# The last tile in parts of 384 and 128 tokens, and 1/rms from a square root and one Newton step

## The chip, the cores and the metric

The program runs on one NeuronCore of a Trainium2 chip. The metric is the device time of one execution in microseconds (us), as the median of several. Engines are named as in the profile: PE (TensorE, matrix products), PEld (its weight loads), DVE (VectorE), ACT (ScalarE), POOL (GpSimd) and SP (SyncE, which here only issues DMAs).

## The reference, cut to what matters

Two decoder layers over 512 tokens of 1024 features: a gated linear recurrence, a convolutional feed-forward block, differential attention over shared keys and values, a second feed-forward block, and a final RMS norm. The change touches only the very end: the last down-projection, the residual sum and the norm.

```
x = x + conv_ffn(rmsnorm(x, norm_ffn[1]), ffn_w_up[1], ...)   # ends in  hidden (512 x 2816) @ w_down (2816 x 1024)
return rmsnorm(x, final_norm)                                 # y = x * rsqrt(mean(x*x, axis=-1) + 1e-6) * g
```

## The kernel before

All arrays lie feature by token: the stream `x` is eight tiles `x[0..7]` of 128 features by T = 512 tokens. Products are in three terms (`mm3`, L104 to L106): each operand is split into a high and a low part (`whi`/`wlo` of a weight, `hh`/`hl` of the hidden layer), and high by high, high by low and low by high are added in one PSUM bank. Each of the three is a matmul with its own weight load.

The second feed-forward block ends in `residual`: for each output tile n it multiplies KF = 22 hidden tiles by 22 blocks of weights, so 66 matmuls of 128x512. The sum is added to `x[n]` (L543), squared on ACT (L148) and accumulated into `acc` on DVE. For the last tile, n = 7, `last_tile` is called. It holds everything that has to follow the last product, and cuts it by tokens so that the first part's norm and stores run under the second part's product:

- `product(half, ks)`: the matmuls of one part for the hidden tiles `ks`. Each part is 66 matmuls, here of 128x256.
- `squares(half)`: residual sum on DVE (L589), squares on ACT (L590), and `scaled` (L585), which multiplies x by the norm's gain into `xg`.
- `sums`: sums over features, as matmuls of a 128-token column block against a column of ones (L183); a column of the result is the sum of one 128-token chunk, a token to a partition. `before` holds the sums over the first seven tiles, already scaled by 1/D with EPS added (L648).
- `factor(half)`: 1/rms on DVE for two columns: the mean square (L603), an integer seed (L604), -0.5 times the mean square (L605), then three Newton steps of `r*mh*r` (L611) and `(u+1.5)*r` (L614), column by column.
- `spread(r)`: each column is turned into a row that all partitions share, by a transpose on PE (L188), into two PSUM banks.
- `finish(half, rb)`: ACT copies one of the two banks to SBUF (L629, `rbc_fin`); DVE multiplies the tiles it has (L634) from the other bank and POOL the rest (L632) into `fin`; each pair of tiles goes to `out` by a DMA (L637), on SP's queue, for the second half on SP's and ACT's in turn.

Inside `manual_schedule(engines=ORDERED)` PE, DVE, ACT and POOL run in the order in which the code is written; SP's DMAs, and how the block is merged with the loop ahead of it, are ordered by the framework's own scheduler. On each engine instructions run in order.

Of the kernel before, what the change touches and what calls it, by code (L numbers as in the profile page):

```python
# [11 lines left out]
F32 = mybir.dt.float32  # L12
F32R = mybir.dt.float32r
I32 = mybir.dt.int32
AF = mybir.ActivationFunctionType
ALU = mybir.AluOpType
# [3 lines left out]
P = 128  # L20
T = 512
D = 1024
KD = D // P
# [3 lines left out]
EPS = 1e-6  # L27
# [9 lines left out]
class Trunk:  # L37
# [527 lines left out]
    def last_tile(self, w_src, ys, kt, acc, out):  # L565

        nc, v, sp = self.nc, self.nc.vector, self.sp
        ws = []
        for k0 in range(0, kt, 8):
            wd = min(8, kt - k0)  # L570
            ws.append(self.weights(w_src[:, k0 * P:(k0 + wd) * P], wd * P))
        x, last = self.x, KD - 1
        t = [slice(half * 256, half * 256 + 256) for half in range(2)]
        ps = [self.bank() for _ in range(2)]
        sq = [sp.tile([P, T], F32, tag="sq", name="sq", bufs=2) for _ in range(2)]

        def product(half, ks):
            for k in ks:
                hi, lo = ws[k // 8]
                c = slice(k % 8 * P, k % 8 * P + P)  # L580
                self.mm3(ps[half][:, :256], (hi[:, c], lo[:, c]), (ys[k][0][:, t[half]], ys[k][1][:, t[half]]),
                         k == 0, k == kt - 1)

        def scaled(n, c):
            nc.scalar.activation(xg[n][:, c], x[n][:, c], AF.Identity, scale=self.gain(5, n))  # L585

        def squares(half):
            c = t[half]
            v.tensor_tensor(x[last][:, c], x[last][:, c], ps[half][:, :256], ALU.add)  # L589
            nc.scalar.activation(sq[half][:, c], x[last][:, c], AF.Square)  # L590
            scaled(last, c)

        def tmp(dt=F32):
            return sp.tile([P, 4], dt, tag="rs", name="rs", bufs=18)[:, :2]

        def sums(src, half):
            return self.sums(src, "mm", (2 * half, 2 * half + 1))[:, 2 * half:2 * half + 2]

        def factor(half):

            ss = sums(sq[half], half)
            ms, mh, i = tmp(), tmp(), tmp(I32)
            v.scalar_tensor_tensor(ms, ss, 1.0 / D, before[half], ALU.mult, ALU.add)  # L603
            v.tensor_scalar(i, ms.bitcast(I32), -0.5, float(0x5F3759DF), ALU.mult, ALU.add)  # L604
            v.tensor_scalar(mh, ms, -0.5, None, ALU.mult)  # L605
            r = i.bitcast(F32)
            for step in range(3):
                u, rn = tmp(), tmp()
                for c in range(2):
                    c = slice(c, c + 1)  # L610
                    v.scalar_tensor_tensor(u[:, c], r[:, c], mh[:, c], r[:, c], ALU.mult, ALU.mult)  # L611
                for c in range(2):
                    c = slice(c, c + 1)
                    v.scalar_tensor_tensor(rn[:, c], u[:, c], 1.5, r[:, c], ALU.add, ALU.mult)  # L614
                r = rn
            return r

        def spread(r):

            both = [self.bank() for _ in range(2)]  # L620
            for rb in both:
                for c in range(2):
                    self.by_column(rb[:, c * P:(c + 1) * P], r[:, c:c + 1])
            return both

        def finish(half, rb):
            by_pool = (KD - 2, KD - 1) if half else (KD - 3, KD - 2, KD - 1)
            rs = sp.tile([P, T], F32, tag="rbc", name="rbc_fin")
            nc.scalar.copy(rs[:, :256], rb[1][:, :256])  # L629
            y = [self.xp.tile([P, 2, 256], F32, tag="xs", name="fin", bufs=2 * KD) for _ in range(KD // 2)]  # L630
            for n in by_pool:
                nc.gpsimd.tensor_tensor(y[n // 2][:, n % 2], xg[n][:, t[half]], rs[:, :256], ALU.mult)  # L632
            for n in range(by_pool[0]):
                v.tensor_tensor(y[n // 2][:, n % 2], xg[n][:, t[half]], rb[0][:, :256], ALU.mult)  # L634
            queues = (nc.sync, nc.scalar if half else nc.sync)
            for n in range(0, KD, 2):
                queues[n // 2 % 2].dma_start(out[n:n + 2, :, t[half]].rearrange("n p t -> p n t"), y[n // 2])  # L637

        with self.tc.manual_schedule(engines=ORDERED):
            xg = [self.xp.tile([P, T], F32, tag="xs", name="xg", bufs=2 * KD) for _ in range(KD)]  # L640
            product(0, range(kt))
            for n in range(last):
                scaled(n, slice(0, T))
            squares(0)
            product(1, range(4))
            before = [tmp() for _ in range(2)]
            for half in range(2):
                v.tensor_scalar(before[half], sums(acc, half), 1.0 / D, EPS, ALU.mult, ALU.add)  # L648
            r = factor(0)
            product(1, range(4, kt - 6))  # L650
            rb = spread(r)
            finish(0, rb)
            product(1, range(kt - 6, kt))
            squares(1)
            finish(1, spread(factor(1)))


    def ffn(self, layer, xs, acc, on_tile, final=None):
# [601 lines left out]
```

## Time and profile before

| | us |
|---|---|
| median of three runs (lowest, highest) | 1266.40 (1265.87, 1267.21) |
| profiled execution, device time | 1266.48 |
| its span, first to last instruction | 1264.7 |
| PE busy in the span | 1237.1 (98%) |
| last tile, first matmul to last: start times in the span | 1236.35 to 1253.81 |
| end of the span after the last matmul of the product began | 10.9 |

Read the last 30 us of the span as two stretches. Up to 1254 PE is never idle, and everything else runs beside it. From then on PE has nothing left but twelve small records, and a chain runs from engine to engine: sum, squares, sums of squares, 1/rms, spread, multiply, store. A row of the timeline gives the start, the time taken, the engine, the line, what is written from what, the shape, how many like it follow one another, and in brackets how long the engine stood idle before it and who ended that. Matmuls overlap in the pipeline, so what one costs is the distance from one start to the next, not its own duration.

### The profile page before, as it was taken

The page shows a single profiled execution, that of the slowest core. Times are in us where ns is not written, and L with a number is a line of the kernel's source. Part 1 is how long each engine was busy: PE and PEld are TensorE (multiplying, and loading weights), DVE is VectorE, ACT ScalarE, POOL GpSimd, SP SyncE. Part 2 cuts the span into 40 slices and gives each one's busy share as a digit, 9 for nine tenths or more (in the row PEclk, how much of TensorE's full clock was granted, in tenths as well). Part 3 has the DMA queues.
Part 4 walks back from the last instruction along what each step waited for, and adds up shares of the span by engine and source line. Part 5 has one row for each costly group of instructions (what it writes and reads, how often), then busy time and mean ns, then how long its engine had stood idle before and what let it go on. Part 6 is the DMA issues. An engine that isn't in the chain of part 4 may idle for free.

```text
span 1264.7 us, 18028 instructions
## 1 busy us (share of the span) xinstructions
PE 1237.1 (98%) x6994; PEld 1045.1 (83%) x6994; DVE 866.1 (68%) x1633; ACT 570.4 (45%) x993; POOL 102.7 (8%) x86
## 2 busy tenths in 40 slices
PE   9999999999999999999999999999999999999997
PEld 7898898778888888888888779788788888888886
DVE  7988978586777777522367988877687777763223
ACT  6455555344444444322235556554454444442221
POOL 0000000020000000000234322201100000000001
PEclk9999999999999999999999999999999999999998
DMA  6224222142333233333332212212233322333322
GB/s 224 71 85 120 84 84 68 36 131 84 100 100 98 89 97 100 92 102 94 96 98 73 73 51 59 84 67 84 83 100 100 100 89 95 100 92 92 99 85 67
DMA packets 38269, 115.36 MB, mean 91 GB/s; under 512 B 3960, under 2 KB 9896, under 8 KB 38184
## 3 DMA queue, kind: packets, MB, share of 16 engines
q1 hardware_dynamic: 37144, 113.27, 29.3%
q8 instruction: 55, 0.90, 0.3%
q10 hardware_dynamic: 1040, 0.94, 0.3%
q14 instruction: 30, 0.25, 0.1%
HBM read 112.09 MB, written 3.68 MB: 92 GB/s over the span
## 4 chain that ended last, share of the span: by engine, by line
PE 58%; issue 30%; DVE 9%; ACT 2%; DMA 0%; POOL 0%; SPq 0%; POOLq 0%; ACTq 0%; DVEq 0%
PE mm L104 16%; PE mm L106 16%; PE mm L105 16%; PE po L1016 1%; DVE kl L868 1%; DVE wlo L60 1%; DVE wlo L770 1%; PE tp L1003 1%; PE sc L104 1%; DVE sd L464 1%; PE sc L105 1%; PE sc L106 1%; ACT whi L59 1%; PE sc L973 0%; PE at L486 0%
## 5 line engine op out<-in xcount | busy, mean ns | idle before, releaser
L104 PE MATMUL mm<-xh,whi 128*128 128x512 f32 x1008 | 399.9, 397 | 0.9 <-ACT whi L59 0.9
L105 PE MATMUL mm<-xl,whi 128*128 128x512 f32 x1008 | 395.5, 392 | 2.1 <-DVE xl L63 2.1
L106 PE MATMUL mm<-xh,wlo 128*128 128x512 f32 x1008 | 395.2, 392 | 0.0
L60 DVE TENSOR_TENSOR wlo<-wst,whi 128x1024 fp32r<-128x1024 f32 x173 | 209.1, 1211 | 149.8 <-ACT whi L59 147.3
L59 ACT CAST whi<-wst 128x1024 fp32r<-128x1024 f32 x173 | 178.1, 1033 | 244.2 <-PE mm L105 191.3
L105 PEld LDWEIGHTS mm<-xl,whi 128*128 128x128 f32 x1008 | 190.9, 189 | 40.4 <-DVE xl L63 3.1
L106 PEld LDWEIGHTS mm<-xh,wlo 128*128 128x128 f32 x1008 | 190.4, 189 | 40.4 <-DVE wlo L60 0.2
L104 PEld LDWEIGHTS mm<-xh,whi 128*128 128x128 f32 x1008 | 191.0, 189 | 39.7 <-issue 1.3
L104 PE MATMUL mm<-hh,whi 128*128 128x512 f32 (+1 forms) x374 | 141.0, 377 | 0.0
L105 PE MATMUL mm<-hl,whi 128*128 128x512 f32 (+1 forms) x374 | 140.8, 377 | 0.0
L106 PE MATMUL mm<-hh,wlo 128*128 128x512 f32 (+1 forms) x374 | 140.8, 376 | 0.0
L676 DVE TENSOR_TENSOR u<-mm,rbc_f 128x512 f32<-128x512 f32 x88 | 60.2, 688 | 73.2 <-PE mm L106 73.2
L105 PEld LDWEIGHTS mm<-hl,whi 128*128 128x128 f32 x374 | 70.4, 188 | 13.0
L104 PEld LDWEIGHTS mm<-hh,whi 128*128 128x128 f32 x374 | 70.4, 188 | 12.9
L106 PEld LDWEIGHTS mm<-hh,wlo 128*128 128x128 f32 x374 | 70.4, 188 | 12.8
L149 POOL TENSOR_TENSOR acc<-acc,sq 128x512 f32<-128x512 f32 x18 | 26.8, 1487 | 664.8 <-ACT sq L148 664.6
L678 ACT ACTIVATE c<-u,pack 128x512 f32<-128x512 f32 x88 | 71.5, 817 | 8.0 <-DVE u L676 3.9
L104 PE MATMUL mm<-whi,xh 128*128 128x256 f32 x256 | 74.1, 290 | 0.0
L59 ACT CAST hh<-c 128x512 fp32r<-128x512 f32 x44 | 27.3, 619 | 103.0 <-DVE c L687 103.0
L105 PE MATMUL mm<-wlo,xh 128*128 128x256 f32 x256 | 72.5, 283 | 0.6 <-DVE wlo L770 0.6
L106 PE MATMUL mm<-whi,xl 128*128 128x256 f32 x256 | 72.4, 283 | 0.0
L680 DVE SCALAR_TENSOR_TENSOR c<-u,pack,c 128x512 f32<-128x512 f32 x88 | 66.1, 751 | 2.7
(262 smaller groups left out, 1712.7 us busy)
## 6 DMA issues: line engine op xcount, KB each, us to landing
wst<-in_w_up_dram SPq DMA_DIRECT2D x88, 512.0 KB, 3.6
wst<-in_w_down_dram SPq DMA_DIRECT2D x32, 512.0 KB, 3.6
wst<-in_w_fqg_dram SPq DMA_DIRECT2D x21, 512.0 KB, 3.9
wst<-in_w_kq_dram SPq DMA_DIRECT2D x16, 512.0 KB, 3.7
wst<-in_w_down_dram SPq DMA_DIRECT2D x16, 384.0 KB, 3.1
wst<-in_w_i_dram SPq DMA_DIRECT2D x8, 512.0 KB, 4.1
wst<-in_w_ao_dram SPq DMA_DIRECT2D x8, 512.0 KB, 4.2
wst<-in_w_v_dram SPq DMA_DIRECT2D x8, 512.0 KB, 3.7
```

The costliest lines, as they stand in the source:

```text
L59: i = nc.scalar.copy(hi, x)
L60: j = nc.vector.tensor_tensor(lo, x, hi.bitcast(F32), ALU.subtract)
L104: mm(out, s[0], m[0], start=start, stop=False)
L105: mm(out, s[0], m[1], start=False, stop=False)
L106: mm(out, s[1], m[0], start=False, stop=stop)
L149: add = lambda engine=nc.vector: engine.tensor_tensor(acc, acc, sq, ALU.add)
L464: v.copy_predicated(dst, m, src)
L676: v.tensor_tensor(u[:, 2:], ps, rb, ALU.mult)
L678: s.activation(c, u[:, 2:], AF.Identity, bias=self.cb[:, layer, n:n + 1], scale=w(2))
L680: v.scalar_tensor_tensor(c, u[:, 0:T], w(0), c, ALU.mult, ALU.add)
L770: v.tensor_tensor(me.w[1], me.st, me.w[0].bitcast(F32), ALU.subtract)
L868: v.tensor_tensor(lo[own, c], k[own], hi[own, c].bitcast(F32), ALU.subtract))
```

## The change

The parts become T - P = 384 tokens (chunks 0, 1 and 2) and P = 128 tokens (chunk 3). 1/rms no longer starts from an integer seed: ACT takes the square root of the mean square (one instruction for each column, with 1/D as its scale and `before` as its bias), DVE the reciprocal, and one Newton step follows. A square root ahead of the products, on a column of `acc`, makes ACT load its table there. The first part's `finish` is cut in three pieces, one ahead of the second part's residual sum, one behind it, and one behind `factor(1)`; each of its tiles is stored by a DMA of its own. The second part's tiles lie in two tiles of four, `last_fin`.

```
-        t = [slice(half * 256, half * 256 + 256) for half in range(2)]
+        t = [slice(0, T - P), slice(T - P, T)]
+        chunks = (0, 1, 2), (3,)
+        width = [T - P, P]
...
+        def stream(part):
+            c = t[part]
+            v.tensor_tensor(x[last][:, c], x[last][:, c], ps[part][:, :width[part]], ALU.add)
+        def squares(part):
+            c = t[part]
+            nc.scalar.activation(sq[part][:, c], x[last][:, c], AF.Square)
+            scaled(last, c)
...
+        def factor(part):
+            ss = sums(sq[part], part)
+            root, r, mh, rn = (tmp(part) for _ in range(4))
+            cols = [slice(n, n + 1) for n in range(len(chunks[part]))]
+            for c in cols:
+                nc.scalar.activation(root[:, c], ss[:, c], AF.Sqrt, scale=1.0 / D, bias=before[part][:, c])
+            v.scalar_tensor_tensor(mh, ss, -0.5 / D, half[part], ALU.mult, ALU.add)
+            v.reciprocal(r, root)
+            u = tmp(part)
+            for c in cols:
+                v.scalar_tensor_tensor(u[:, c], r[:, c], mh[:, c], r[:, c], ALU.mult, ALU.mult)
+            for c in cols:
+                v.scalar_tensor_tensor(rn[:, c], u[:, c], 1.5, r[:, c], ALU.add, ALU.mult)
+            return rn
...
+                if not part:
+                    nc.sync.dma_start(out[n, :, t[part]], y)
+                elif n % 2:
+                    queue = nc.scalar if n in by_pool else nc.sync
+                    queue.dma_start(out[n - 1:n + 1, :, t[part]].rearrange("n p t -> p n t"),
+                                    last_fin[n // 4][:, n % 4 - 1:n % 4 + 1])
...
+            nc.scalar.activation(tmp(1), acc[:, 0:1], AF.Sqrt)
...
             product(1, range(4, kt - 6))
-            rb = spread(r)
-            finish(0, rb)
+            rb, rs = spread(r, 0)
+            finish(0, rb, rs, (6, 7, 0, 1))
             product(1, range(kt - 6, kt))
+            stream(1)
             squares(1)
-            finish(1, spread(factor(1)))
+            finish(0, rb, rs, (2, 3))
+            r = factor(1)
+            finish(0, rb, rs, (4, 5))
+            rb, rs = spread(r, 1)
+            finish(1, rb, rs, (6, 7, 0, 1, 2, 3, 4, 5))
```

On PE the list is as long as before, with other widths. Around the sums it read so before (`hh`, `hl` the hidden tiles, `acc` and `sq` the squares):

```order
L104 MATMUL mm<-hh_8609,whi 128x256
L105 MATMUL mm<-hl_8610,whi 128x256
L106 MATMUL mm<-hh_8609,wlo 128x256
L183 MATMUL mm<-ones,acc 128x1 x4
L183 MATMUL mm<-ones,sq 128x1 x2
L104 MATMUL mm<-hh_8611,whi 128x256
```

and so now:

```order
L104 MATMUL mm<-hh_8609,whi 128x128
L105 MATMUL mm<-hl_8610,whi 128x128
L106 MATMUL mm<-hh_8609,wlo 128x128
L183 MATMUL mm<-ones,acc 128x1 x4
L183 MATMUL mm<-ones,sq 128x1 x3
L104 MATMUL mm<-hh_8611,whi 128x128
```

The 66 products ahead of these rows' part are 384 columns wide instead of 256, the 66 of this part 128, with one sum more among them; the first spread is six transposes instead of four, the last two instead of four.

On DVE, from the second part's residual sum to the end, before (`x_79` is the last tile of x, `rs` the small columns of 1/rms):

```order
L589 TENSOR_TENSOR x_79<-x_79,mm 128x256
L603 SCALAR_TENSOR_TENSOR rs<-mm,rs 128x2
L604 TENSOR_SCALAR rs<-rs 128x2
L605 TENSOR_SCALAR rs<-rs 128x2
L611 SCALAR_TENSOR_TENSOR rs<-rs 128x1 x2
L614 SCALAR_TENSOR_TENSOR rs<-rs 128x1 x2
L611 SCALAR_TENSOR_TENSOR rs<-rs 128x1 x2
L614 SCALAR_TENSOR_TENSOR rs<-rs 128x1 x2
L611 SCALAR_TENSOR_TENSOR rs<-rs 128x1 x2
L614 SCALAR_TENSOR_TENSOR rs<-rs 128x1 x2
L634 TENSOR_TENSOR fin<-xg,mm 128x256 x6
```

and now (`fin_11022` and `fin_11023` are the two tiles of `last_fin`):

```order
L591 TENSOR_TENSOR x_79<-x_79,mm 128x128
L638 TENSOR_TENSOR fin<-xg,mm 128x384 x2
L612 SCALAR_TENSOR_TENSOR rs<-mm,rs 128x1
L613 RECIPROCAL rs<-rs 128x1
L616 SCALAR_TENSOR_TENSOR rs<-rs 128x1
L618 SCALAR_TENSOR_TENSOR rs<-rs 128x1
L638 TENSOR_TENSOR fin<-xg,mm 128x384 x2
L638 TENSOR_TENSOR fin_11022<-xg,mm 128x128 x4
L638 TENSOR_TENSOR fin_11023<-xg,mm 128x128 x2
```

Fifteen small instructions became four, and four multiplications of the first part now stand between the last product and the second part's own.

On ACT, the end of the list before (the multiplications by the gain, `xg`, of the first seven tiles stood one by one behind each tile's squares):

```order
L148 ACTIVATE sq<-x_78 128x512
L585 ACTIVATE xg<-x_78,gains 128x512
L590 ACTIVATE sq<-x_79 128x256
L585 ACTIVATE xg<-x_79,gains 128x256
L629 COPY rbc_fin<-mm 128x256
L590 ACTIVATE sq<-x_79 128x256
L585 ACTIVATE xg<-x_79,gains 128x256
L629 COPY rbc_fin<-mm 128x256
```

and now, from the last of the seven gains on:

```order
L587 ACTIVATE xg<-x_78,gains 128x512
L595 ACTIVATE sq<-x_79 128x384
L587 ACTIVATE xg<-x_79,gains 128x384
L611 ACTIVATE rs<-mm,rs 128x1 x3
L628 COPY rbc_fin<-mm 128x384
L595 ACTIVATE sq<-x_79 128x128
L587 ACTIVATE xg<-x_79,gains 128x128
L611 ACTIVATE rs<-mm,rs 128x1
L628 COPY rbc_fin<-mm 128x128
```

All seven `xg` of the first tiles now follow one another behind the table load and the square root on `acc`, since that one waits for the complete `acc`. On SP's queue six DMAs of two tiles became eight of one tile of 384 tokens and three of two tiles of 128; ACT's has one instead of two.

More of the change, by code (lines that the diff above doesn't have):

```diff
@@ L572, in last_tile, with product @@
         x, last = self.x, KD - 1
-        t = [slice(half * 256, half * 256 + 256) for half in range(2)]
+        t = [slice(0, T - P), slice(T - P, T)]
+        chunks = (0, 1, 2), (3,)
+        width = [T - P, P]
         ps = [self.bank() for _ in range(2)]
         sq = [sp.tile([P, T], F32, tag="sq", name="sq", bufs=2) for _ in range(2)]
-        def product(half, ks):
+        def product(part, ks):
             for k in ks:
@@ L580, in product @@
                 c = slice(k % 8 * P, k % 8 * P + P)
-                self.mm3(ps[half][:, :256], (hi[:, c], lo[:, c]), (ys[k][0][:, t[half]], ys[k][1][:, t[half]]),
+                self.mm3(ps[part][:, :width[part]], (hi[:, c], lo[:, c]), (ys[k][0][:, t[part]], ys[k][1][:, t[part]]),
                          k == 0, k == kt - 1)
@@ L585, in scaled @@
             nc.scalar.activation(xg[n][:, c], x[n][:, c], AF.Identity, scale=self.gain(5, n))
[L587 to L590, printed above, removed]
-            scaled(last, c)
[L593 to L616, printed above, removed]
@@ L618, in spread, with tmp, sums @@
-        def spread(r):
+        def stream(part):
[4 more added lines that the diff above has]
+            nc.scalar.activation(sq[part][:, c], x[last][:, c], AF.Square)
+            scaled(last, c)
+        def tmp(part):
+            return sp.tile([P, 4], F32, tag="rs", name="rs", bufs=18)[:, :len(chunks[part])]
+        def sums(src, part):
+            own = chunks[part]
+            return self.sums(src, "mm", own)[:, own[0]:own[-1] + 1]
@@ L620, in spread @@
+        def spread(r, part):
             both = [self.bank() for _ in range(2)]
             for rb in both:
[L622 to L627, printed above, removed]
-            rs = sp.tile([P, T], F32, tag="rbc", name="rbc_fin")
[L629 to L637, printed above, removed]
+                for n in range(len(chunks[part])):
+                    self.by_column(rb[:, n * P:(n + 1) * P], r[:, n:n + 1])
+            rs = sp.tile([P, T], F32, tag="rbc", name="rbc_fin")
+            nc.scalar.copy(rs[:, :width[part]], both[1][:, :width[part]])
+            return both[0], rs
@@ new lines, in finish @@
+        def finish(part, rb, rs, ns):
+            w = width[part]
+            for n in ns:
+                y = last_fin[n // 4][:, n % 4] if part else fin[n][:, :w]
+                if n in by_pool:
+                    nc.gpsimd.tensor_tensor(y, xg[n][:, t[part]], rs[:, :w], ALU.mult)
+                else:
+                    v.tensor_tensor(y, xg[n][:, t[part]], rb[:, :w], ALU.mult)
+                if not part:
[4 more added lines that the diff above has]
+                                    last_fin[n // 4][:, n % 4 - 1:n % 4 + 1])
@@ L639, in last_tile @@
+        by_pool = (KD - 2, KD - 1)
         with self.tc.manual_schedule(engines=ORDERED):
+            nc.scalar.activation(tmp(1), acc[:, 0:1], AF.Sqrt)
             xg = [self.xp.tile([P, T], F32, tag="xs", name="xg", bufs=2 * KD) for _ in range(KD)]
+            fin = [self.xp.tile([P, T], F32, tag="xs", name="fin", bufs=2 * KD) for _ in range(KD)]
+            last_fin = [sp.tile([P, 4, P], F32, tag="res", name="fin0", bufs=1),
+                        sp.tile([P, 4, P], F32, tag="acc", name="fin1")]
@@ L643, in last_tile @@
                 scaled(n, slice(0, T))
+            stream(0)
             squares(0)
             product(1, range(4))
-            before = [tmp() for _ in range(2)]
-            for half in range(2):
-                v.tensor_scalar(before[half], sums(acc, half), 1.0 / D, EPS, ALU.mult, ALU.add)
+            before, half = [tmp(0), tmp(1)], [tmp(0), tmp(1)]
+            for part in range(2):
+                ss = sums(acc, part)
+                v.tensor_scalar(before[part], ss, 1.0 / D, EPS, ALU.mult, ALU.add)
+                v.tensor_scalar(half[part], before[part], -0.5, None, ALU.mult)
             r = factor(0)
             product(1, range(4, kt - 6))
-            rb = spread(r)
-            finish(0, rb)
+            rb, rs = spread(r, 0)
+            finish(0, rb, rs, (6, 7, 0, 1))
             product(1, range(kt - 6, kt))
+            stream(1)
             squares(1)
-            finish(1, spread(factor(1)))
+            finish(0, rb, rs, (2, 3))
[3 more added lines that the diff above has]
+            finish(1, rb, rs, (6, 7, 0, 1, 2, 3, 4, 5))
     def ffn(self, layer, xs, acc, on_tile, final=None):
```

## Prediction

> **What bounds the kernel now.** I read the page first, then the timeline of PE over the last 30 us, then that of the other engines after PE's last product, then groups of instructions for prices, the DMA view, and last the busy time and granted clock by stretches. On the page, the busy shares and the granted clock in 40 slices:
>
> ```profile
> PE 1237.1 (98%) x6994; PEld 1045.1 (83%) x6994; DVE 866.1 (68%) x1633; ACT 570.4 (45%) x993; POOL 102.7 (8%) x86
> PEclk9999999999999999999999999999999999999998
> ```
>
> PE is the bound to the end of the last product, and DVE, ACT and POOL have room. So any time added to PE's stream counts in full, and the rest of the time is what follows it. The timeline of PE in the last tile:
>
> ```profile
> 1236.35 0.28 PE L104 MATMUL mm<-hh,whi 128*128 128x256 f32 x1
> ...
> 1244.26 0.28 PE L104 MATMUL mm<-hh,whi 128*128 128x256 f32 x1
> ...
> 1245.70 0.95 PE L183 MATMUL mm<-ones,acc 128*128 128x1 f32 x8
> 1246.51 0.58 PE L183 MATMUL mm<-ones,sq 128*128 128x1 f32 x4
> 1246.96 0.36 PE L104 MATMUL mm<-hh,whi 128*128 128x256 f32 x1
> ...
> 1251.35 0.60 PE L188 MATMUL mm<-pack,rs 128*128 128x128 f32 x4
> 1251.70 0.36 PE L104 MATMUL mm<-hh,whi 128*128 128x256 f32 x1
> ...
> 1253.81 0.28 PE L106 MATMUL mm<-hh,wlo 128*128 128x256 f32 x1
> 1255.11 0.61 PE L183 MATMUL mm<-ones,sq 128*128 128x1 f32 x4 [1.02 <-ACT sq L590]
> 1257.61 1.12 PE L188 MATMUL mm<-pack,rs 128*128 128x128 f32 x4 [1.89 <-DVE rs L614]
> ```
>
> The first half's 66 products take 1244.26 - 1236.35 = 7.91 us, 0.120 each. Twelve records of sums take 1.26, 0.105 each (a sum makes two), four transposes 0.35. The last product ends at 1254.09; after it only the chain is left, 10.6 us to the span's end at 1264.7. Its steps on the other engines:
>
> ```profile
> 1254.13 0.42 DVE L589 TENSOR_TENSOR x<-x,mm 128x256 f32<-128x256 f32 x1 [0.62 <-PE mm L106]
> 1254.64 0.42 ACT L590 ACTIVATE sq<-x 128x256 f32<-128x256 f32 x1 [2.29 <-DVE x L589]
> 1255.76 0.16 DVE L603 SCALAR_TENSOR_TENSOR rs<-mm,rs 128x2 f32<-128x2 f32 x1 [1.21 <-PE mm L183]
> ...
> 1256.22 0.35 DVE L611 SCALAR_TENSOR_TENSOR rs<-rs 128x1 f32<-128x1 f32 x2
> ...
> 1256.68 0.34 DVE L611 SCALAR_TENSOR_TENSOR rs<-rs 128x1 f32<-128x1 f32 x2
> ...
> 1258.33 2.08 DVE L634 TENSOR_TENSOR fin<-xg,mm 128x256 f32<-128x256 f32 x6 [0.66 <-PE mm L188]
> ...
> 1260.65 0.41 ACTq L637 DMA_DIRECT2D out_dram<-fin  x1
> ```
>
> Each step starts 0.03 to 0.09 us after the one that it waits for, so the chain is dense; the largest piece is 1/rms, from 1255.76 to the transposes at 1257.61, then the six multiplications and the stores.
>
> **The change part by part: PE's stream.** Products of 128 and 384 columns, each with its own weight load, stand one after another in the attention's scores:
>
> ```profile
> 681.08 0.28 PE L973 MATMUL sc<-kl,qs 128*128 128x128 f32 x1
> 681.20 0.27 PE L972 MATMUL sc<-kh,qs 128*128 128x128 f32 x1
> 681.31 0.27 PE L973 MATMUL sc<-kl,qs 128*128 128x128 f32 x1
> 681.42 0.44 PE L104 MATMUL mm<-xh,whi 128*128 128x512 f32 x1
> ...
> 692.62 0.34 PE L972 MATMUL sc<-kh,qs 128*128 128x384 f32 x1
> ...
> 693.15 0.33 PE L973 MATMUL sc<-kl,qs 128*128 128x384 f32 x1
> ```
>
> At 128 columns a step is 0.34/3 = 0.113 us, hardly less than the 0.120 at 256: the weight load sets it. At 384 it is 0.53/3 = 0.177. A column costs (0.177 - 0.120)/128, so 128 columns stream in about 0.055, half of the 0.113. Then the first part costs 66 x (0.177 - 0.120) = +3.76, the second 66 x (0.113 - 0.120) = -0.46, one sum more 2 x 0.105 = +0.21, two transposes more +0.18. Sum +3.7 us: PE's last product ends near 1257.8. Lower end: a 128 step of 0.06, below; upper end: 0.12 for each, +4.2.
>
> The Trainium skill, TensorE: Matmul & The Clock Gate, section Back-to-back issue gap, gives about 81 ns for a sustained stream of weight loads and 128-column matmuls. No run here shows that; the rows show 0.113. By the page's 81 ns (an estimate) PE's stream would grow by 1.6 instead of 3.7 us.
>
> **The end.** After the last product:
> - Residual sum: 0.42 at 256 columns against 0.69 at 512 (L543, below), so 0.29 at 128: -0.13. The square by the same slope, -0.11. One sum instead of two: -0.22.
> - 1/rms took 1.85 from L603 to the transposes. Now: ACT's root 0.17 (the two-column activation below; 0.3 as upper end, since no row has one with a bias column), two hand-overs of 0.05, 0.08 behind L612, the reciprocal 0.16, one Newton step of 0.46 at most (1256.22 to 1256.68), 0.05 to PE. About 1.0, so -0.85. The first part's two multiplications ahead of it on DVE (two of about 0.47, from the 0.33 distance at 256) are done before the root arrives, 1.4 us after PE's end.
> - Spread to the last DMA's issue took 3.05 (1257.61 to 1260.65). Now DVE has two 384-wide multiplications left when 1/rms is done, 0.95, which cover the two transposes, then six of 0.20: 2.2 in all, -0.85.
>
> ```profile
> L543 DVE TENSOR_TENSOR x<-x,mm 128x512 f32<-128x512 f32 x15 | 10.3, 688 | 26.6 <-PE mm L106 26.6
> L992 DVE RECIPROCAL r<-sums 128x1 f32<-128x1 f32 x32 | 5.0, 156 | 0.0
> L740 ACT ACTIVATE lme<-mm 128x2 f32<-128x2 f32 x1 | 0.2, 173 | 0.0
> L740 ACT ACT_TABLE_LOAD x1 | 1.3, 1283 | 0.0
> L585 ACT ACTIVATE xg<-x,gains 128x512 f32<-128x512 f32 x7 | 5.0, 707 | 0.0
> ```
>
> The table load (1.28) and the seven `xg` (5.0 together), now in a row behind `acc`, cost nothing: the first part's product, 11.7 us on PE, covers them with over 4 us to spare. If it didn't, the first part's squares would be late, and next PE's sums.
>
> The stores. First the DMA view from 1250 to 1265 in 40 slices, with the SP queue's packets of 1 KB, then SP's queue from 2.9 to 3.3 us, where nearly all packets have 512 bytes:
>
> ```profile
> GB/s 0 0 44 0 0 0 0 0 0 248 328 344 355 331 341 350 350 150 0 0 0 0 0 0 0 0 87 347 341 325 341 361 339 347 300 8 0 0 0 0
> q1 hardware_dynamic: 1632, 1.57, 31.2%
> ...
> q1 hardware_dynamic: 224, 0.13, 102.4%
> ```
>
> A 1 KB packet took 0.312 x 16 x 15/1632 = 0.046 us, a 512-byte one 1.024 x 16 x 0.4/224 = 0.029. The data end at about 1263.15, 2.5 after the last issue and 1.5 before the span's end, and flow at a steady rate from 1260.0: the queue binds there. Now the last 1024 packets have 512 bytes: 64 on each of 16 engines, 1.9 us instead of 2.9, behind two 384-token tiles still under way; data end 2.05 after the last issue, -0.45. Upper end, if 512 bytes cost as much as 1 KB: +0.6 instead. SP's other stores wait for POOL and DVE well before; nobody waits for them.
>
> The end shrinks by 0.13 + 0.11 + 0.22 + 0.85 + 0.85 + 0.45 = 2.6 us. **The sum**: +3.7 - 2.6 = +1.1 on the profiled execution's 1266.48, which stands 0.1 above the median of 1266.40. So about 1267.4 by the median, if PE's clock stays as it is. 0.2% of this kernel is 2.5 us, about what a measurement can tell from no change: 1263.9 to 1268.9 counts as none.
>
> **The rivals.** First, *PE's clock falls in the second part*. The granted clock by stretches, with the rows that tell what PE did there:
>
> ```profile
> 16.98:20.39 3.41, 1.85 (x9) 1.00 0.19 41
> 235.43:238.84 3.41, 3.41 (x10) 0.50 0.00 0
> 1252.59:1256.00 3.41, 2.11 (x17) 1.00 0.76 253
> 1256.00:1259.42 3.42, 1.12 (x4) 0.50 0.16 55
> ...
> 18.44 0.39 PE L106 MATMUL mm<-xh,wlo 128*128 128x512 f32 x1
> ...
> 0.99 3.78 PE L255 MATMUL at<-ones 128*128 128x128 f32 x16 [0.99 <-POOL ones L217]
> ...
> 6.32 0.58 PE L104 MATMUL mm<-xh,whi 128*128 128x512 f32 x1
> ```
>
> At 1256.00 the clock dropped to half, after a stretch in which PE was busy for 2.11 of 3.41 us, more than the 1.85 from 16.98 on, which kept full clock. What sets the two apart is streaming: products ran to 1253.92 at 0.107 of 0.120, 0.35 of the stretch, against 0.46 (to 18.65, dense 512-column products). The sums stream one column and hardly count. In the changed kernel a stretch that holds the 14 records of sums (1.5 us) and else 128-column products, half of whose 0.113 streams, comes to about 0.27: by this rule the clock falls for most positions of the stretches, four in five. The price: half clock takes 0.21 a product (sixteen in 3.78). If it comes back after one stretch, about 14 products are lost, +1.6: 1269.0. If it doesn't, some 39 products and six transposes cost 0.10 more each, +4.6: 1272.0. For the second: at the start PE streamed from 0.99 on, and a 512-column product at 6.32 still took 0.58; half-filled stretches are less than that. Against both: it may be enough for PE to have anything in flight, the drain behind each sum included, which adds 0.05 to a record and then sets these two stretches only 0.03 apart, on the other side of what the change would have. The point from which it decides is a share between 0.35 and 0.46.
>
> The Trainium skill, TensorE: Matmul & The Clock Gate, Part 1, has the clock fall after at least one idle window of 3.4 us. PE idles nowhere that long in the second part, so by that rule the clock stays, as in the forecast; but the drop at 1256.00 came behind a stretch with work in it, and there the measurement decides.
>
> Second, *the weight loads hide*. After a long product the load of the next is already done, and L973 can follow L972 by 0.06 us. If the reordering held that over 66 products, the second part would take 3.5 us less, and the time be 1263.8. The rows speak against it: in the same run of four the later steps are 0.11 to 0.12. By the page's 81 ns above, 1265.3 (an estimate).
>
> **How the numbers follow.** Clock kept, steps as in the rows: 0.45, 1267.4, its own range 1265.8 to 1268.9. Clock falls and stays: 0.30, 1272.0; falls for one stretch: 0.12, 1269.0, half of it past 1268.9. Loads hide: 0.08, half of it below 1263.9. The other 0.05, effects on the work ahead of the last tile, which the change leaves as it was but for ACT's order, go to both sides. So slower 0.40, within 0.2% 0.51, faster 0.09. The range, 1265.2 to 1272.4, leaves out the hidden loads and the upper part of a clock that stays low.
>
> **What the profile after would show.** 66 steps of 0.173 to 0.18 and then of 0.11 on PE, its last product's end at 1257.5 to 1258, and 7.9 us from there to the span's end. Steps of 0.21 and a clock of 0.50 in the second part would make it wrong upward; steps below 0.09, downward. A wait on PE at the sums or the first spread would mean that ACT's list or the root is late; stores that end over 2.6 us after their last issue, that 512-byte packets cost more than a read's.

## The result, and the profile after

Six executions of each kernel on the same chip: before 1266.84 us in the median (1265.87 to 1267.98), after 1271.68 (1269.96 to 1274.59). The measured ratio is 1.0042, with a 95% interval of 1.0030 to 1.0054 (the two medians alone give 1.0038): slower by some 0.4%. The profiled execution took 1271.92 us, 5.44 more than the profiled one of before. The busy shares and the granted clock on the page:

```profile
PE 1240.5 (98%) x6994; PEld 1048.9 (83%) x6994; DVE 865.9 (68%) x1618; ACT 572.8 (45%) x999; POOL 102.4 (8%) x85
PEclk9999999999999999999999999999999999999997
```

Only the last slice of the clock tells anything: a 7 where it was an 8. The timeline of PE in the last tile shows why, by the distance from one start to the next:

```profile
1236.94 0.33 PE L104 MATMUL mm<-hh,whi 128*128 128x384 f32 x1
...
1248.23 0.33 PE L106 MATMUL mm<-hh,wlo 128*128 128x384 f32 x1
1248.40 0.22 PE L104 MATMUL mm<-hh,whi 128*128 128x128 f32 x1
1248.46 0.27 PE L105 MATMUL mm<-hl,whi 128*128 128x128 f32 x1
...
1249.69 1.00 PE L183 MATMUL mm<-ones,acc 128*128 128x1 f32 x8
1250.55 0.81 PE L183 MATMUL mm<-ones,sq 128*128 128x1 f32 x6
1251.22 0.31 PE L104 MATMUL mm<-hh,whi 128*128 128x128 f32 x1
1251.37 0.28 PE L105 MATMUL mm<-hl,whi 128*128 128x128 f32 x1
...
1253.38 0.27 PE L105 MATMUL mm<-hl,whi 128*128 128x128 f32 x1
...
1253.64 0.42 PE L104 MATMUL mm<-hh,whi 128*128 128x128 f32 x1
...
1256.85 1.50 PE L188 MATMUL mm<-pack,rs 128*128 128x128 f32 x6
...
1261.66 0.41 PE L106 MATMUL mm<-hh,wlo 128*128 128x128 f32 x1
1262.86 0.58 PE L183 MATMUL mm<-ones,sq 128*128 128x1 f32 x2 [0.78 <-ACT sq L595]
1264.51 0.69 PE L188 MATMUL mm<-pack,rs 128*128 128x128 f32 x2 [1.06 <-DVE rs L618]
```

The first part's steps are (1248.23 - 1236.94)/65 = 0.174 us, the second part's (1253.38 - 1251.37)/18 = 0.112 up to 1253.5, and from 1253.64 on 0.213. The list holds no wait until the last product is done, so PE simply ran at half its pace. (What PE has left after the last product are four small records; in before they were eight, four of sums and four of transposes, not the twelve of the text ahead.) By stretches of 3.41 us (time, PE busy with its count, PEld, DVE, ACT and POOL likewise, then the granted clock):

```profile
1246.71:1250.13 3.42, 3.42 (x28) 3.42 (x26) 0.56 (x1) 0.88 (x2) 0.00 (x0) 1.00 0.00 0
1250.13:1253.54 3.41, 3.41 (x33) 3.41 (x33) 1.47 (x12) 0.72 (x4) 0.00 (x0) 1.00 0.00 0
1253.54:1256.95 3.41, 3.41 (x19) 3.41 (x18) 0.00 (x0) 0.00 (x0) 0.00 (x0) 0.50 0.02 5
1256.95:1260.37 3.42, 3.42 (x18) 3.42 (x18) 1.02 (x2) 0.48 (x1) 1.43 (x2) 0.50 0.16 58
```

The clock fell behind a stretch in which PE and its weight loads were busy for all of the 3.41 us. What that stretch lacked is columns: from 1251.22 on it holds 21 products of 128 columns, 21 x 0.055 = 1.15 us of streaming, a share of 0.34 (0.33 with 0.053 a product: 512 columns take 0.426 us at half clock, from 236.00 to 238.13 in the trace of before, so 0.213 at full clock and 0.053 for a quarter of them). And it stayed low through two more stretches full of such products, six transposes among them. This is the first rival of the prediction; what it cost is in the table further down.

The other engines, at the start of the tile and after the last product:

```profile
1238.51 1.28 ACT L648 ACT_TABLE_LOAD   x1
...
1239.91 4.39 ACT L587 ACTIVATE xg<-x,gains 128x512 f32<-128x512 f32 x7
1249.25 0.52 ACT L595 ACTIVATE sq<-x 128x384 f32<-128x384 f32 x1 [4.95 <-DVE x L591]
...
1263.48 0.26 ACT L611 ACTIVATE rs<-mm,rs 128x1 f32<-128x1 f32 x1 [0.38 <-PE mm L183]
...
1266.89 0.44 SPq L643 DMA_DIRECT2D out_dram<-fin  x1
```

The table load and the seven `xg` are done at 1244.30, and ACT then stands idle for 4.95 us: they cost nothing. 1/rms takes 1264.51 - 1263.48 = 1.03 us, the spread to the last store's issue 1266.89 - 1264.51 = 2.38, and from the last product's end (1262.07) to the span's end (1270.1) it is 8.0 us.

Where a number needs to be free of what happens earlier in the kernel, take the length of the last tile, from its first product to the span's end. It is read from one profiled execution each and has no interval. Before: 1264.7 - 1236.35 = 28.35 us; after: 1270.1 - 1236.94 = 33.16. So 4.8 of the 5.44 us arose in the last tile; the tile also started 0.59 later, for a reason that the last section gives.

### The profile page after: what moved, and what is told of

Same layout as the page of the kernel before. It is cut to its first block, busy times and chain, and to the rows that moved or that the text cites. A ratio compares the mean times of both kernels' runs of the same rounds, so it can differ in the third digit from the quotient of the medians.

```text
span 1270.1 us, 18027 instructions
## 1 busy us (share of the span) xinstructions
PE 1240.5 (98%) x6994; PEld 1048.9 (83%) x6994; DVE 865.9 (68%) x1618; ACT 572.8 (45%) x999; POOL 102.4 (8%) x85
## 4 chain that ended last, share of the span: by engine, by line
PE 85%; DVE 10%; ACT 3%; issue 1%; DMA 0%; SPq 0%; DVEq 0%; ACTq 0%
PE mm L104 26%; PE mm L106 26%; PE mm L105 26%; DVE wlo L790 1%; DVE wlo L60 1%; PE po L1036 1%; DVE kl L888 1%; PE tp L1023 1%; ACT whi L787 1%; PE sc L104 1%; PE sc L105 1%; DVE xl L63 1%; PE sc L106 1%; DVE sd L464 1%; ACT whi L59 1%
## 5 line engine op out<-in xcount | busy, mean ns | idle before, releaser
L106 PE MATMUL mm<-hh,wlo 128*128 128x512 f32 (+2 forms) x374 | 143.4, 383 | 0.0
L104 PE MATMUL mm<-hh,whi 128*128 128x512 f32 (+2 forms) x374 | 143.3, 383 | 0.0
L105 PE MATMUL mm<-hl,whi 128*128 128x512 f32 (+2 forms) x374 | 143.3, 383 | 0.0
```

The lines of the kernel that those rows point to most:

```text
L104: mm(out, s[0], m[0], start=start, stop=False)
L105: mm(out, s[0], m[1], start=False, stop=False)
L106: mm(out, s[1], m[0], start=False, stop=stop)
```

## The experiments

The theory ("clock"): the share of a 3.41 us stretch in which columns stream decides whether the clock falls, and what the clock took is the loss. Rivals: ScalarE's root and its table load; the wider and narrower steps; the sums as such.

**e1, the split without the root.** The new parts, order and stores, but 1/rms as before (a line of three dots stands for lines left out, here and below):

```
-            for c in cols:
-                nc.scalar.activation(root[:, c], ss[:, c], AF.Sqrt, scale=1.0 / D, bias=before[part][:, c])
...
+            v.tensor_scalar(i, ms.bitcast(I32), -0.5, float(0x5F3759DF), ALU.mult, ALU.add)
+            for step in range(3):
...
```

> The parts of 384 and 128 tokens and the new order of the last steps, but 1/rms as before: the bit trick and three Newton steps on VectorE, no root and no table load on ScalarE. Theory clock: the change lost its time because TensorE's granted clock falls behind the sums in the second part and stays at 0.50, whatever 1/rms is made from. Then it falls here as well, the products after it take 0.21 us each, and only the 1/rms at the very end is longer, 1.85 instead of 1.03 us: 1271.7 + 0.8 = 1272.5 us, mean clock 0.989 to 0.992. Rival, ScalarE's root: the table load of 1.28 us and the hand-overs to ScalarE and back delay PE or the end. Then this one stands near the forecast with the longer 1/rms, 1268.2 us.

1273.79 us, ratio to before 1.0061 (1.0049 to 1.0073). The last tile took 1272.3 - 1237.61 = 34.7 us, 1.5 more than the changed kernel's: 0.8 for the longer 1/rms, and the fall came 0.8 us earlier in the tile, so that seven more products took 0.213 instead of 0.112, 0.7 in all. The stretches:

```profile
1250.00:1253.42 3.42, 3.42 (x33) 3.42 (x32) 1.60 (x14) 0.95 (x2) 0.00 (x0) 1.00 0.00 0
1253.42:1256.83 3.41, 3.41 (x19) 3.41 (x17) 1.01 (x11) 0.00 (x0) 0.00 (x0) 0.50 0.02 5
```

The clock falls with no root anywhere, in the same way. So the split brings it down.

**e2, the root without the split.** Two halves of 256 tokens, with the order and stores of before; `factor`, which makes 1/rms, with the root and one Newton step, and the table load ahead of the tile.

> Two halves of 256 tokens as before, with the order and the stores of before, but 1/rms from ScalarE's root and one Newton step, and the table load at the head of the last tile. Theory clock: 256-column products stream 0.107 of 0.120 us, the clock stays at 1.00 in the second half, PE's last product ends where it did, and 1/rms is 0.85 us shorter: 1266.8 - 0.85 = 1266.0 us. Rival, ScalarE's root: over 1268 us.

1265.77 us beside 1265.95, ratio 0.9999 (0.9989 to 1.0009): no difference that this measurement can tell, the 0.85 expected being inside the interval. The trace resolves it. The last tile took 1265.6 - 1238.15 = 27.45 us, 0.9 less than before's, and the clock stayed at 1.00 past the last product and the spread, to 1260.4:

```profile
1255.61 0.28 PE L106 MATMUL mm<-hh,wlo 128*128 128x256 f32 x1
...
1258.74 0.66 PE L188 MATMUL mm<-pack,rs 128*128 128x128 f32 x4 [1.23 <-DVE rs L611]
```

From the last product's start to the spread it is 3.13 us here, 3.80 before; the rest is the spread itself, which in before fell into the half clock behind 1256.00. In this pair of traces the root is worth 0.7 us, with no loss anywhere; the times can't show so little.

**e3, the second part with redundant columns.** If columns are what is missing, more of them should make the kernel faster:

```
-                self.mm3(ps[part][:, :width[part]], (hi[:, c], lo[:, c]), (ys[k][0][:, t[part]], ys[k][1][:, t[part]]),
+                m = slice(T - 256, T) if part else t[0]
+                self.mm3(ps[part][:, :m.stop - m.start], (hi[:, c], lo[:, c]), (ys[k][0][:, m], ys[k][1][:, m]),
...
```

> The changed kernel, but the second part's products have 256 columns instead of 128: tokens 256 to 511, of which only the last 128 are read. The work is redundant, the instructions are as many. Theory clock (what counts is the share of a 3.41 us stretch in which columns stream): a stretch that holds all 14 records of sums still streams 0.89 x 1.9 / 3.41 = 0.50, the clock stays at 1.00 to the last product, 33 half-clock products at +0.10 and the transposes at +0.10 each are saved, about 4.0 us, and 66 steps of 0.120 instead of 0.111 cost 0.6: 1271.7 - 3.4 = 1268.3 us, faster with more work. Rival (the sums as such, or the parts' weight loads, bring the clock down; or the clock isn't where the time went): no gain and 0.3 to 0.6 us more for the wider products, 1272 us or over.

1267.93 us, ratio 1.0014 (1.0006 to 1.0023), where the changed kernel had 1.0042: 0.28% of 1266, 3.5 us, came back by streaming twice the columns in the second part. The last tile took 1264.5 - 1234.84 = 29.66 us. The stretch that holds all the sums, and the next one:

```profile
1247.45:1250.87 3.42, 3.42 (x32) 3.42 (x31) 1.39 (x12) 1.30 (x5) 0.00 (x0) 1.00 0.00 0
1250.87:1254.28 3.41, 3.41 (x32) 3.41 (x31) 0.23 (x3) 0.00 (x0) 0.00 (x0) 1.00 0.02 5
```

PE and PEld are as busy as in the changed kernel, the instructions are as many and the sums stand in the same place; only the columns differ, a share of 0.48 instead of 0.33. The theory holds, and neither the sums as such nor the number of weight loads is the cause.

**e5, the sums of `acc` moved into the first part's product.** Eight of the fourteen records go to where 384-column products surround them:

```
-            product(0, range(kt))
+            product(0, range(kt - 4))
+            of_acc = [sums(acc, part) for part in range(2)]
+            product(0, range(kt - 4, kt))
...
```

> The changed kernel, but the sums of acc (8 of the 14 records) stand within the first part's product, ahead of its last 12 products, where 384-column products surround them; the six records of the first part's own squares stay between 128-column products. PE's work is the same. Theory clock: a stretch that holds these six (0.67 us) streams 0.48 x 2.74 / 3.41 = 0.385, between the largest share behind which the clock fell (0.354) and the smallest behind which it stayed (0.426). If the bound lies below 0.385, the clock stays at 1.00 and the time is 1271.7 - 4.0 = 1267.7 us; if above, it falls as in the changed kernel, 1271.7. Rival (the clock isn't where the time went): 1271.7 whether or not the clock falls.

1272.50 us, ratio 1.0048 (1.0035 to 1.0062), last tile 33.9: no better.

```profile
1248.94:1252.36 3.42, 3.42 (x32) 3.31 (x31) 1.70 (x13) 1.59 (x5) 0.00 (x0) 1.00 0.00 0
1252.36:1255.77 3.41, 3.41 (x19) 3.41 (x18) 0.03 (x1) 0.00 (x0) 0.00 (x0) 0.50 0.02 5
```

The six records left, and a pause ahead of them, lowered this stretch to a share of 0.36 instead of the 0.385 that I had worked out, and the clock fell. So the bound lies above 0.36. Half-filled products left no room for these six records and the pause.

**e4, 192 columns instead of 256.** The same edit as e3 with `T - 192`.

> The changed kernel with second-part products of 192 columns (tokens 320 to 511, the first 64 redundant). Theory, the weight load sets the 128-column step (0.111 us, of which 0.053 streams): 64 columns more stream 0.080 and fit beneath the load, so the step stays at 0.111 to 0.115, at no cost. With them a stretch that holds all 14 sum records streams 0.72 x 1.9 / 3.41 = 0.40, one that holds the last 10 of them 0.50; the clock fell behind 0.357 and less and stayed behind 0.426 and more, so for nearly all positions it should stay at 1.00: 1271.3 - 4.0 = 1267.3 us on this scale, 0.6 less than with 256 columns. Rival (a step costs by its columns, 0.095 or so at 192 after 0.111 at 128 is excluded, 0.145 by the slope from 128 to 384): 66 x 0.03 = 2 us more. Rival (only dense columns keep the clock): falls, 1271.5.

1268.12 us, ratio 1.0005 (0.9996 to 1.0014). The step, and the stretch that holds all the sums:

```profile
1254.48 0.27 PE L105 MATMUL mm<-hl,whi 128*128 128x192 f32 x1
...
1254.70 0.28 PE L104 MATMUL mm<-hh,whi 128*128 128x192 f32 x1
...
1259.25 0.28 PE L106 MATMUL mm<-hh,wlo 128*128 128x192 f32 x1
```

```profile
1250.34:1253.75 3.41, 3.41 (x33) 3.41 (x32) 1.08 (x8) 1.59 (x5) 0.00 (x0) 1.00 0.00 0
```

The step, (1254.70 - 1254.48)/2 = 0.11 us (0.112 over 34 steps), is the same at 192 columns as at 128: something that doesn't go by columns sets it, and half again as many are free. That it is the weight load is argued from one row: behind a 384-column product, under which the next load fits, the second 128-column product starts 0.06 after the first (1248.40 and 1248.46 in the changed kernel). The stretch holds 17 products of 192 columns, 17 x 0.080 = 1.36 us or 0.40 of its time, and the clock stayed. The last tile took 1267.4 - 1238.35 = 29.05 us. This is the changed kernel as the forecast had it, with the clock kept: 0.7 us above before.

**e6, wide products only after the fall.** 256 columns from the eleventh of the second part's 22 hidden tiles on (and in its first), 128 around the sums. It ran once, so it has no interval.

> The changed kernel with 256-column products only from the 11th of the 22 steps of the second part on (and in its first step); the products around the sums stay at 128 columns. So the clock should fall behind the sums as in the changed kernel. Theory A (a stream that is half filled keeps a fallen clock down, a dense one brings it back after one full stretch): the clock rises to 1.00 after one or two stretches of 3.41 us, the last 18 to 25 products take 0.120 again, and the time is about 1270. Theory B (the clock stays down for a fixed time or to the end once it fell this late): 0.50 to the end, 36 products at 0.21 to 0.24, 1272 us.

1271.17 us, between the two theories' times; the trace tells them apart. The last tile took 1269.4 - 1238.53 = 30.9 us, 2.3 less than the changed kernel's.

```profile
1251.72:1255.14 3.42, 3.42 (x32) 3.42 (x32) 1.48 (x12) 0.72 (x4) 0.00 (x0) 1.00 0.00 0
1255.14:1258.55 3.41, 3.41 (x18) 3.41 (x17) 0.00 (x0) 0.00 (x0) 0.00 (x0) 0.50 0.02 5
1258.55:1261.96 3.41, 2.99 (x26) 2.79 (x24) 1.40 (x4) 0.48 (x2) 1.98 (x2) 1.00 0.18 66
```

The clock fell behind the sums and came back after one stretch of 256-column products. In the changed kernel, at the same place, 128-column products kept it down. So a half-filled stream neither held the clock over the sums nor brought it back.

**e7 to e9, columns in the waits of the whole kernel.** If the share decides everywhere, the falls ahead of the last tile can be had as well. In e2 six 512-column products that nobody reads are put where PE waits:

```
+    def filler(self, out, x, n=6):
+        for _ in range(n):
+            self.nc.tensor.matmul(out, x[:, 0:P], x, start=True, stop=True)
```

> Two halves and the root of e2, and at three places of the kernel where PE waits for 2.1 us in every trace (before the sums at 20.9, before the last head's output at 234.0, and in the second FFN's first products at 893.4 us of the kernel before) six 512-column products more, whose results nobody reads, 1.36 us each time. Theory (a stretch's streaming share decides, everywhere in the kernel): the clock fell behind these waits in four to five of the six traces each, and a fall costs 1.3 to 1.6 us there (PE was 1.28 us later after a fall at 21.3, 1.63 after one at 894). The filler adds 1.36/3.41 = 0.40 to the share, the three falls go, and the time is e2's less 0.67 x 4.5 = 3.0: about 1262.9 us, mean clock 0.995 or above. Rival (idle time as such, or power, decides; or the waits grow by the filler): no gain, or 1 to 4 us more.

1263.13 us beside 1266.94, ratio 0.9970 (0.9959 to 0.9981): faster, but not all for the reason given. The third group had landed behind the transposes at 904.5, where PE doesn't wait; the wait at 887.4 stayed and the clock fell behind it at 890.3. And the group ahead of the last head's output had moved other work: 14 rows of real products now filled that wait. So two more kernels, one with the third group moved into its wait, one that also leaves out the second group, so that PE's order is that of e2 but for twelve unread products.

> e7 with the third group of six unread products moved: in e7 it stood behind the transposes at 904.5, where PE doesn't wait, and the wait at 887.4 to 889.5 stayed, with the clock at 0.50 behind it. Now it stands ahead of the product that waits there (the first FFN product's seventh step), within that wait. Theory (streaming share): 1.36 us of unread work on the path goes, and the fall at 890, seen in five of seven traces at 1.63 us, goes too: e7's ratio 0.997 less (1.36 + 1.1)/1266 = 0.995, 1260.8 us beside a before of 1266.9. Rival (the clock falls by idle time as such): the 1.36 us only, 0.996, 1261.8 us, with 0.50 still behind the wait.

> e8 without the group before the last head's output. In e7 and e8 that group also moved the last head's transposed products 14 rows later on PE, so that real work filled the wait of 2.2 us; without it PE's order is that of e2 but for the 12 unread products in the waits at 18 and 888, and every other engine's order is that of e2. So this one tests unread work alone. Theory (streaming share): the falls behind these two waits go; they were seen in four and five of seven traces, at 1.28 and 1.63 us, so e2's time less 0.6 x 1.28 + 0.7 x 1.63 = 1.9 us: ratio 0.9999 - 0.0015 = 0.9984, 1264.9 us beside a before of 1266.9. Rival (no effect of work that nobody reads): e2's ratio, 0.9999.

e8: 1260.54 us (1260.09 to 1260.86) beside 1267.09, ratio 0.9946 (0.9933 to 0.9958). e9: 1262.38, ratio 0.9962 (0.9949 to 0.9976). Around the wait in the second feed-forward block, first two stretches and the wait of before, then the same wait and two stretches of e8:

```profile
890.78:894.19 3.41, 1.34 (x5) 0.86 (x5) 3.17 (x3) 0.72 (x2) 1.37 (x1) 1.00 0.27 95
894.19:897.60 3.41, 3.41 (x9) 2.67 (x8) 1.35 (x2) 1.03 (x2) 0.00 (x0) 0.50 0.15 59
```

```profile
890.60 0.39 PE L106 MATMUL mm<-xh,wlo 128*128 128x512 f32 x1
890.83 0.50 PE L104 MATMUL mm<-xh,whi 128*128 128x512 f32 x1
893.40 0.50 PE L105 MATMUL mm<-xl,whi 128*128 128x512 f32 x1 [2.07 <-DVE xl L63]
```

```profile
886.91 0.39 PE L106 MATMUL mm<-xh,wlo 128*128 128x512 f32 x1
887.14 1.52 PE L186 MATMUL mm<-xh 128*128 128x512 f32 x6
888.50 0.39 PE L104 MATMUL mm<-xh,whi 128*128 128x512 f32 x1
889.73 0.50 PE L105 MATMUL mm<-xl,whi 128*128 128x512 f32 x1 [0.85 <-DVE xl L63]
```

```profile
885.71:889.12 3.41, 3.17 (x15) 2.29 (x13) 3.29 (x4) 1.89 (x3) 2.68 (x5) 1.00 0.10 32
889.12:892.53 3.41, 2.80 (x12) 2.34 (x13) 2.51 (x4) 1.25 (x2) 0.01 (x1) 1.00 0.41 144
```

The wait ends where it did, 2.82 us after the product ahead of it (2.80 in before), so the unread products cost nothing, and the fall is gone; in e8's trace the clock holds 1.00 from 5.1 to 1250.9 us, past the last product. e8's gain is not that of unread work alone, since the moved rows of e7 are in it. e9's order on PE is that of e2 but for the twelve products. It gained 0.38%, 4.7 us, where I had expected 0.16%. Its profiled run shows 2.6 of them: 0.9 in the last tile, 1.6 behind the wait above, the fall that didn't come. How often the falls come in runs without a profile isn't known, so the rest stays open. e8 and e9 beat both kernels.

## Why the prediction was right and wrong

The time, 1271.68, lies in the range and within 0.4 us of the first rival, "falls and stays, 1272.0". The forecast was another case, 1267.4 with the clock kept, and that one missed by 4.3 us: the range held because the rival's price was in it. So the step that failed is the weight on the cases, 0.45 to 0.30, and not a term of the sum.

| step | predicted | measured |
|---|---|---|
| 384-column step | 0.177 | 0.174 |
| 128-column step | 0.113 | 0.112, and 0.112 at 192 columns (e4) |
| PE's stream, clock kept | +3.7 | e4: (1259.53 - 1238.35) - (1254.09 - 1236.35) = +3.4 |
| 1/rms | 1.0 | 1.03 (e1, the old one: 1.8) |
| spread to the last store's issue | 2.2 | 2.38 |
| last product to the span's end | 7.9 | 8.0, and 7.9 in e4 |
| data's end behind the last store's issue | 2.05 | about 2.0 |
| the sum, clock kept | +1.1 | e4: 29.05 - 28.35 = +0.7 |
| the clock falls and stays | +4.6 more | 33.16 - 29.05 = +4.1 |

The table load, `xg` and the stores cost nothing, as said. The weight loads did not hide (the second rival): 0.112 from the second product on. One price was right though its rows don't give it: sixteen products from 0.99 to 4.71 are 0.23 each at half clock, not the 0.21 that was written, and 0.213 was measured. And the widths' difference, 0.177 - 0.120, is 0.057 for 128 columns, not 0.055; measured, 0.053.

What went wrong in the weights. The rule of the streaming share was there, with its bounds of 0.35 and 0.46 and a stretch of 0.27 to be expected, and I wrote that it would bring the clock down in four positions of five. I gave the case that it stays down 0.30, because I let one other reading, that anything in flight is enough, stand beside it. That reading rested on 0.05 us added to each record of a sum, which no row had measured, and the quoted rows spoke against it: the stretch behind which the clock fell was the busier one, 2.11 against 1.85 us. The four other falls in the trace of before couldn't decide it, since PE was busy for under 1.4 us in each of their stretches. A doubt was due; more weight for the reading with the unmeasured correction than for the rule without one was not. All four traces with 128-column products around the sums (the changed kernel, e1, e5, e6) have the fall, and e4 and e3, with more columns in the same time, don't, though PE had something in flight all through these stretches in every one of the six. The comparison with the start ("half-filled stretches are less than that") also held: the clock stayed down at a share of 0.50.

The Trainium skill, TensorE: Matmul & The Clock Gate, Part 1, has the clock fall after at least one idle window of about 3.4 us and rise after one busy window of that length. The free-running window of 3.41 us agrees with these traces. The two conditions don't: the clock fell behind a stretch in which PE was busy for 3.41 of 3.41 us, and did not rise after the next, just as busy. There the measurement decides: in these traces the share of columns tells the stretches apart, and busy time does not. The same page's section Back-to-back issue gap gives about 81 ns for a stream of weight loads and 128-column products; these traces have 0.112.

## What to carry to other kernels

When a tile is cut narrower, ask first what share of PE's time still streams columns: here a product with its own weight load took 0.112 us at 128 and at 192 columns alike, and the sums beside 128-column products halved the clock. Columns that nobody needs were free there, and so were unread products inside a wait: e4 won 0.4% back from the changed kernel, and e9 0.4% from before, with a root that by itself (e2) made no difference that could be measured. A balanced cut (256 and 256) kept the clock to the last product with no such help, and with the root it had the shortest last tiles, 27.45 us (e2) to 27.7 (e8).

## What the runs showed of the hardware

In the last tile the share has a narrow bound. Nearly all columns there are of split products, at 0.42 ns each (half of the 0.426 us that 512 take at half clock). Where sums stand between products, the stretches behind which the clock fell had a share of 0.27 (e1), 0.33 (the changed kernel), 0.34 (e6) and 0.36 (e5), the lowest of those that kept it 0.40 (e4) and 0.48 (e3). Busy time does not order them: in all six PE was busy for the whole stretch.

Over the whole of the eleven traces the same bound comes out if a column of a transpose or of another product of unsplit operands is counted double. The clock then fell behind 45 stretches of 3.41 us, each with a share of at most 0.38, and of those with more than 0.39 it fell behind none; one at 0.37 kept it. It came back behind stretches of 0.78 and more at half clock, and stayed down at 0.71 and less. The doubling is chosen to fit and not measured: counted once, six stretches of 0.32 to 0.34 kept the clock while others of up to 0.36 lost it.

The stretches lie at another place in every execution. Within a trace the falls are whole stretches apart (21.33 and 236.37 in the changed kernel, 63 of them), from trace to trace they are not (the first is at 21.21 in e1, at 22.93 in e6). That moves the start of the last tile from trace to trace, here by 0.59 us: in the changed kernel's the clock fell at 21.33, in before's it didn't, and after that point PE ran 1.28 us later; the attention added 0.9, for a reason that wasn't looked for; and in before's the clock fell at 894.19, in the changed kernel's not, which gave 1.63 back. It is likely a part of the scatter: e8, without these falls, ran within 0.8 us, before, on the same chip, within 4.6.
